# Latent attention: sine tables through DRAM in two transfers, its opening in one written order, four order lists as two blocks

## The chip, the cores and the metric

The kernel runs on one core of one Trainium2 chip. The metric is the device time of one execution in microseconds (us). The core has five engines that take their own instructions in order and wait for each other by semaphores: PE (TensorE, matmuls; its weight loads are listed as PEld), DVE (VectorE), ACT (ScalarE), POOL (GpSimd) and SP (SyncE, which only issues transfers). Transfers (DMAs) are issued here by SP and POOL and run on 16 DMA engines. Matmuls read SBUF and write PSUM, which has eight banks.

## What is computed

One layer of a streaming encoder. The part at hand is multi-head latent attention over 1024 prompt rows and 32 sample rows, 8 heads, cut from the reference:

```
q = (rms_norm(q_lat, g_q_lat) @ w_uq).reshape(B, T, H_A, NOPE + ROPE)      # 384 -> 8 x (64 + 32)
q_rope = apply_rope(q[..., NOPE:], cos[:, None, :], sin[:, None, :])
k_rope = apply_rope(k_r, cos, sin)
k_nope, v = c_kv @ w_uk, c_kv @ w_uv                                       # 256 -> 8 x 64 each
s = (einsum('bqhd,bshd->bhqs', q_nope, k_nope) + einsum('bqhr,bsr->bhqs', q_rope, k_rope)) * 96 ** -0.5
mask = (kpos[None, :] // 64) <= (qpos[:, None] // 64)
p = softmax(where(mask, s, -1e30)); o = einsum('bhqs,bshd->bqhd', p, v)
```

Stick-breaking attention, its projection `o_b @ w_proj_b`, the gates, the merge and a convolutional feed-forward follow or stand around it. Every product of float32 operands is made of three matmuls (`mm3`): each operand is split into a high half, written by ACT (`hi`, L68), and a low half, the rest, written by DVE (`lo`, L71), and high·high, low·high and high·low are added in PSUM.

## The kernel before

**Stages.** `run` calls the stages in turn: projections, stick-breaking attention (`stage_sb`), the latents (`stage_lat`, L1243), latent attention (`stage_mla`, L1378), merge, feed-forward. A planner orders each engine's instructions by data, free buffers and its own estimate of durations. Inside a `manual_schedule` region the engines named there keep the order in which the code issues; SP and POOL stay with the planner.

**Latents.** `lat_rstd` (L1201) works out 1/rms of the query latent, sends it to DRAM and back as nine columns (`cols`, five transfers on POOL, L1218 and L1220), by which the scores' exponentials are scaled. The key rope rows are rotated and spread over `KRp` in twelve pieces (L1355, POOL).

**Opening of `stage_mla`.** The scaled cosine and sine tables are loaded into `tc` and `KSm`, 128 partitions of four equal parts, by twelve SP transfers (L1385, L1387). For head pair 0, `expansion(p)` returns steps: `I`/`i` split the weights; `z` (nine steps) makes the rotary products of four heads, `B` (six) multiplies them by the tables (L1446) and sends them to DRAM (`rqc`, `rqs`, L1448), from where rows of each head come back (L1455) into its query tile; `x` (nine) makes the other query products and `X`/`K` copy them (L1465 on DVE, L1463 on ACT); `y` (four) makes the keys, `H`/`L` their high and low halves, alternating between the two heads; `J`/`j` are the query tile's high half QH and low half QL (L1469, L1473); `Z` copies the sample's columns. `values` makes the value tiles of four heads. `proj_b` is the other branch's projection, done meanwhile: `O` splits its input `ob`, `U` loads a weight, `W`/`w` split it, `f` is a fill of three matmuls, `G` stores a result. All this opening is outside a manual region: the planner orders it.

**The four blocks.** `mla_attend` (L898) plays one list of items per head pair in a manual region for PE, ACT and DVE: `ORDER_0`, `ORDER_A`, `ORDER_A`, `ORDER_L` for pairs 0 to 3. An item is a letter and a place: in `S2.1a`, 2 is the unit (0 to 3 are the blocks of 256 rows of the pair's first head, 4 to 7 those of the second in falling size), 1 its half of 128 rows, `a` a part of the keys. `S` scores (one of three PSUM banks), `M`, `m`, `n` the scaled maximum, `E` the exponential into a row tile (five buffers), `s`, `R`, `C` or `c` the normalisation, `T` the turn (transposes to one of two banks), `h`, `v` its halves, `V` weights by values (one bank), `o`, `p` the output. Letters alone are fills: those of `proj_b`, and those of the next pair's expansion, so that each list ends with its last keys and queries. Pair 3 has the sample's attention (`Y`) and the split of its output (`q`, `r`). Between pairs 1 and 2 the planner orders the sample's latents and the values of the second four heads.

Of the kernel before, what the change touches and what calls it, by code (L numbers as in the profile page):

```python
# [44 lines left out]
class K:  # L45
# [777 lines left out]
    def sb_weights(self, pieces, w):  # L823
# [26 lines left out]
    ORDER_0 = """  # L850
        S0.0 S0.1 S1.0 W f M0.0 n0.0 f M0.1 n0.1 M1.0 n1.0 f E0.0 f E0.1 w f E1.0 S1.1 G R0.0 R0.1 R1.0 c0.0
        S2.0a C0.1 c1.0 M1.1 n1.1 S2.0b M2.0a T0.0 E1.1 f M2.0b h0.0 f R1.1 m2.0 C1.1 E2.0a f v0.0 E2.0b S2.1a G
        s2.0 S2.1b R2.0 M2.1a c2.0 V0.0 M2.1b S3.0a o0 m2.1 E2.1a p0 T1.1 M3.0a E2.1b T1.0 f s2.1 R2.1 W S3.0b
        C2.1 h1.1 S3.1a w h1.0 v1.1 f2 v1.0 f M3.0b V1.1 G M3.1a V1.0 T2.2 m3.0 o1 T2.1 E3.0a p1 f h2.2 f h2.1
        v2.2 f E3.0b S3.1b v2.1 V2.2 s3.0 M3.1b T2.0 R3.0 V2.1 m3.1 c3.0 S4.0a h2.0 f M4.0a E3.1a f v2.0 f G f
        E3.1b S4.0b s3.1 R3.1 V2.0 C3.1 S4.1a o2 M4.0b f p2 T3.3 m4.0 M4.1a G T3.2 E4.0a f h3.3 f h3.2 v3.3 f
        E4.0b S4.1b v3.2 V3.3 s4.0 M4.1b T3.1 R4.0 V3.2 m4.1 c4.0 S5.0a h3.1 T3.0 M5.0a f E4.1a v3.1 f I f2 V3.1
        S5.0b G i h3.0 f2 E4.1b f G f v3.0 z z z B B z z z B B z z z B B x s4.1 S5.1a M5.0b R4.1 m5.0 V3.0 C4.1
        E5.0a x E5.0b M5.1a x o3 s5.0 p3 T4.3 R5.0 T4.2 X K c5.0 S5.1b h4.3 S6.0 h4.2 M5.1b x v4.3 x v4.2 T4.1
        m5.1 M6.0 n6.0 E5.1a V4.3 h4.1 V4.2 E5.1b x v4.1 E6.0 T4.0 s5.1 X K f R5.1 R6.0 W V4.1 C5.1 S6.1 G w  # L860
        h4.0 T5.2 c6.0 v4.0 S7.0 h5.2 x M6.1 n6.1 T5.1 v5.2 E6.1 V4.0 M7.0 n7.0 h5.1 x R6.1 C6.1 o4 T5.0 v5.1
        E7.0 x h5.0 p4 S7.1 R7.0 X K c7.0 y v5.0 J V5.2 M7.1 n7.1 V5.1 Z E7.1 j V5.0 T6.1 o5 T6.0 h6.1 R7.1 p5 y
        C7.1 h6.0 v6.1 v6.0 H H L V6.1 V6.0 L T7.0 o6 h7.0 p6 v7.0 y V7.0 y o7 p7 H H L L Z J j
    """.split()

    ORDER_A = """
        S0.0 S0.1 S1.0 W f M0.0 n0.0 f M0.1 n0.1 M1.0 n1.0 f E0.0 f E0.1 w f E1.0 S1.1 G R0.0 R0.1 R1.0 c0.0
        S2.0a C0.1 c1.0 M1.1 n1.1 S2.0b M2.0a T0.0 E1.1 f M2.0b h0.0 f R1.1 m2.0 C1.1 E2.0a f v0.0 E2.0b S2.1a G
        s2.0 S2.1b R2.0 M2.1a c2.0 V0.0 M2.1b S3.0a o0 m2.1 E2.1a p0 T1.1 M3.0a E2.1b T1.0 f s2.1 R2.1 W S3.0b
        C2.1 h1.1 S3.1a w h1.0 v1.1 f2 v1.0 f M3.0b V1.1 G M3.1a V1.0 T2.2 m3.0 o1 T2.1 E3.0a p1 f h2.2 f h2.1  # L870
        v2.2 f E3.0b S3.1b v2.1 V2.2 s3.0 M3.1b T2.0 R3.0 V2.1 m3.1 c3.0 S4.0a h2.0 f M4.0a E3.1a f v2.0 f G f
        E3.1b S4.0b s3.1 R3.1 V2.0 C3.1 S4.1a o2 M4.0b f p2 T3.3 m4.0 M4.1a G T3.2 E4.0a f h3.3 f h3.2 v3.3 f
        E4.0b S4.1b v3.2 V3.3 s4.0 M4.1b T3.1 R4.0 V3.2 m4.1 c4.0 S5.0a h3.1 T3.0 M5.0a f E4.1a v3.1 f I f2 V3.1
        S5.0b G i h3.0 f2 E4.1b f G f v3.0 x s4.1 S5.1a M5.0b R4.1 m5.0 V3.0 C4.1 E5.0a x E5.0b M5.1a x o3 s5.0
        p3 T4.3 R5.0 T4.2 X K c5.0 S5.1b h4.3 S6.0 h4.2 M5.1b x v4.3 x v4.2 T4.1 m5.1 M6.0 n6.0 E5.1a V4.3 h4.1
        V4.2 E5.1b x v4.1 E6.0 T4.0 s5.1 X K f R5.1 R6.0 W V4.1 C5.1 S6.1 G w h4.0 T5.2 c6.0 v4.0 S7.0 h5.2 x
        M6.1 n6.1 T5.1 v5.2 E6.1 V4.0 M7.0 n7.0 h5.1 x R6.1 C6.1 o4 T5.0 v5.1 E7.0 x h5.0 p4 S7.1 R7.0 X K c7.0
        y v5.0 J V5.2 M7.1 n7.1 V5.1 Z E7.1 j V5.0 T6.1 o5 T6.0 h6.1 R7.1 p5 y C7.1 h6.0 v6.1 v6.0 H H L V6.1
        V6.0 L T7.0 o6 h7.0 p6 v7.0 y V7.0 y o7 p7 H H L L Z J j
    """.split()  # L880

    ORDER_L = """
        S0.0 S0.1 S1.0 W f M0.0 n0.0 f M1.0 n1.0 f M0.1 n0.1 E0.0 f E1.0 w f E0.1 Y G S1.1 R0.0 R1.0 R0.1 Y C0.1
        S2.0a c0.0 c1.0 M1.1 n1.1 S2.0b M2.0a E1.1 Y M2.0b T0.0 Y R1.1 f m2.0 C1.1 S2.1a h0.0 E2.0a v0.0 f E2.0b
        Y M2.1a s2.0 R2.0 V0.0 c2.0 S2.1b Y T1.1 o0 M2.1b T1.0 h1.1 p0 S3.0a h1.0 m2.1 v1.1 f q v1.0 E2.1a f
        V1.1 r E2.1b M3.0a f G W Y s2.1 R2.1 C2.1 w V1.0 T2.2 o1 Y h2.2 p1 v2.2 q r T2.1 Y V2.2 h2.1 T2.0 v2.1 f
        Y f2 h2.0 Y V2.1 G S3.0b v2.0 S3.1a M3.0b Y m3.0 M3.1a E3.0a V2.0 E3.0b f2 o2 s3.0 S3.1b Y R3.0 p2 c3.0
        S4.0a M3.1b Y q f M4.0a Y f G r f m3.1 Y E3.1a E3.1b s3.1 R3.1 C3.1 S4.0b Y S4.1a M4.0b Y m4.0 M4.1a
        E4.0a T3.3 f Y E4.0b T3.2 h3.3 s4.0 S4.1b R4.0 h3.2 v3.3 c4.0 S5.0a v3.2 T3.1 M4.1b V3.3 h3.1 M5.0a V3.2
        m4.1 v3.1 f E4.1a T3.0 E4.1b f V3.1 h3.0 s4.1 R4.1 Y G C4.1 v3.0 T4.3 T4.2 h4.3 Y h4.2 v4.3 v4.2 V3.0 Y  # L890
        f o3 T4.1 p3 f Y f2 h4.1 V4.3 Y q V4.2 G v4.1 S5.0b Y r M5.0b T4.0 Y V4.1 m5.0 h4.0 S5.1a E5.0a v4.0 Y f
        E5.0b M5.1a f Y S5.1b s5.0 R5.0 c5.0 Y M5.1b m5.1 E5.1a E5.1b s5.1 V4.0 R5.1 Y C5.1 S6.0 o4 S6.1 p4 M6.0
        n6.0 q Y r E6.0 T5.2 M6.1 n6.1 S7.0 h5.2 Y f E6.1 R6.0 M7.0 n7.0 T5.1 v5.2 c6.0 f R6.1 C6.1 h5.1 T5.0
        V5.2 E7.0 v5.1 h5.0 S7.1 G R7.0 v5.0 T6.1 c7.0 f h6.1 M7.1 n7.1 V5.1 v6.1 E7.1 V5.0 R7.1 T6.0 C7.1 o5 f
        p5 h6.0 f q V6.1 v6.0 G T7.0 r V6.0 h7.0 o6 v7.0 p6 q V7.0 r o7 p7 q r
    """.split()

    def mla_attend(self, order, score, V, out, fill):  # L898
        nc, vec = self.nc, self.nc.vector
        tiles, banks, stats = {}, {}, {}  # L900
        common = self.sums(V, out, tiles)
        for x in order:
            k, x = x[0], x[1:]
            if k in "fGWwxyzXKBJjZHLIiYqr":
                for _ in range(int(x or 1)):
                    fill(k)
                continue
# [10 lines left out]
            if k == "S":  # L918
                if not j:
# [281 lines left out]
    def lat_rstd(self, ps, n, cols=None):  # L1201
# [14 lines left out]
        if cols is not None:  # L1216
            d = d.rearrange("q c -> (q c)")
            nc.gpsimd.dma_start(cols[:, :8], d[:TP].rearrange("(b p) -> p b", p=P))  # L1218
            for q in range(4):
                nc.gpsimd.dma_start(cols[32 * q : 32 * q + 32, 8:9], d[TP:].rearrange("(p b) -> p b", b=1))  # L1220
            return
# [21 lines left out]
    def stage_lat(self):  # L1243
# [13 lines left out]

        lp = self.tc.alloc_tile_pool(name="lt", bufs=2, reuse_waits="tile")
# [119 lines left out]
    def stage_mla(self):  # L1378
# [5 lines left out]
        for j in range(0, P, 32):  # L1384
            nc.sync.dma_start(tc_[j : j + 32], a["k_ropeq"][64:96])  # L1385
            for d in (0, 16):
                nc.sync.dma_start(ts_[j + d : j + d + 16], a["k_ropeq"][112 - d : 128 - d])  # L1387
# [7 lines left out]
        def expansion(p, banks="mm"):  # L1395
# [85 lines left out]
            def keys():  # L1481
                for c0 in (0, 512):
                    ps = self.bank(next(banks))
                    c = slice(c0, c0 + 512)
                    for e in range(2):
                        kb.append((ps[64 * e : 64 * e + 64], e, c))
# [4 lines left out]
            def k_high():  # L1491
                ps, e, c = kb[k_done[0]]
                k_done[0] += 1
                self.hi(KHs[e][0:64, c], ps)

            def k_low():
                ps, e, c = kb[k_done[1]]
                k_done[1] += 1
                self.lo(KLs[e][0:64, c], ps, KHs[e][0:64, c])

            k_done = [0, 0]
# [3 lines left out]
                        J=q_high, j=q_low, Z=q_sample, H=k_high, L=k_low), QH, QL  # L1505

        def values(hf, raw, gt):
# [3 lines left out]
            for t in range(0, 8, 2):  # L1511
                ps = self.bank(gt.split()[t // 2 % len(gt.split())])
                for j in range(2):
                    tk = slice((t + j) * P, (t + j + 1) * P)
                    for k in range(2):
                        self.mm3(ps[:, j * 256 : j * 256 + 256], self.CPh[k][:, tk], self.CPl[k][:, tk],
                                 h[:, k * 256 : k * 256 + 256], l[:, k * 256 : k * 256 + 256], k == 0, k == 1)
                pv = ps.rearrange("r (j q h d) -> r j q h d", j=2, q=2, h=2)
                for q in range(2):
# [32 lines left out]
        for k in "JjZ":  # L1552
            steps[k]()
# [1121 lines left out]
```

## Time and profile before

| | us |
|---|---|
| three runs: median (lowest, highest) | 1716.35 (1715.44, 1718.22) |
| the profiled execution | 1719.44 |
| its span, first to last instruction | 1717.7 |
| PE busy in the span | 1654.9 |
| first matmul of `stage_mla` | 571.87 after the span's start |
| first score of pair 0 | 600.66 |
| end of pair 3, as cut here | 861.20 |

Times in the profile count from the span's start. Ends of matmuls are modelled, so busy time of PE says little of its rate; the spacing of starts says more. A wait is put down to the instruction whose semaphore came last.

### The profile page before, as it was taken

To read this page: it belongs to the slowest core of one execution; us is meant where nothing else is said; L and a number is where in the kernel's file an instruction comes from. 1 tells how busy PE (TensorE), PEld (TensorE's weight loads), DVE (VectorE), ACT (ScalarE), POOL (GpSimd) and SP (SyncE) were. 2 spreads that over 40 slices of the span, in tenths; PEclk is the share of its full clock that TensorE was granted. 3 is DMA by queue.
4 is the path that set the end of the run, shared out by engine and by line. 5 is a ranking of instruction groups with operands and counts; after the bars stand their busy time and mean duration, and the time that the engine had idled before them with its cause. 6 is when DMAs were issued, how large, how long until landed. Compare 5 with 4: busy or idle time off the path is not lost. (4 is left out here: it accounts for less than half of the span.)

```text
span 1717.7 us, 30277 instructions
## 1 busy us (share of the span) xinstructions
PE 1654.9 (96%) x11592; PEld 1508.9 (88%) x11592; DVE 1273.6 (74%) x2140; ACT 1007.2 (59%) x1945; POOL 297.9 (17%) x578
## 2 busy tenths in 40 slices
PE   5999999999999798999999999999999999999997
PEld 3999999999998687897889789999999999977885
DVE  4865788988864568777776779887787787787455
ACT  4544687888865457777773476444444444544442
POOL 3113212121110411110100121211121111110013
PEclk8999999999999999999999999999999999999999
DMA  9345966576432623221274531423333333697643
GB/s 331 101 134 182 295 206 178 174 195 179 137 111 72 157 71 99 67 84 53 67 263 149 172 127 57 143 93 130 132 105 132 131 110 132 231 333 244 210 138 120
DMA packets 192849, 259.54 MB, mean 151 GB/s; under 512 B 22270, under 2 KB 131200, under 8 KB 192704
## 3 DMA queue, kind: packets, MB, share of 16 engines
q1 hardware_dynamic: 171888, 198.97, 37.3%
q0 software_dynamic: 20592, 58.55, 9.8%
q8 instruction: 91, 1.49, 0.4%
q14 instruction: 54, 0.44, 0.1%
q10 hardware_dynamic: 224, 0.09, 0.0%
HBM read 190.02 MB, written 66.74 MB: 149 GB/s over the span
## 5 line engine op out<-in xcount | busy, mean ns | idle before, releaser
L68 ACT ACTIVATE wh<-wr 128x1024 fp32r<-128x1024 f32 (+3 forms) x151 | 130.2, 864 | 229.6 <-PE s L2129 84.1
L71 DVE TENSOR_TENSOR wl<-wr,wh 128x1024 fp32r<-128x1024 f32 (+3 forms) x151 | 148.4, 986 | 83.4 <-ACT wh L68 80.8
L75 PE MATMUL mm<-hh,wh 128*128 128x352 f32 x456 | 152.6, 335 | 0.0
L76 PE MATMUL mm<-hl,wh 128*128 128x352 f32 x456 | 148.9, 327 | 0.4 <-DVE hl L333 0.4
L77 PE MATMUL mm<-hh,wl 128*128 128x352 f32 x456 | 148.4, 326 | 0.0
L2128 PE MATMUL mm<-T,wh 128*128 128x256 f32 (+1 forms) x376 | 108.1, 288 | 0.0
L2130 PE MATMUL mm<-T,wl 128*128 128x256 f32 (+1 forms) x376 | 107.1, 285 | 0.4 <-DVE wl L71 0.2
L2129 PE MATMUL mm<-T,wh 128*128 128x256 f32 (+1 forms) x376 | 106.6, 284 | 0.0
L2130 PE MATMUL s<-T,wl 128*128 128x256 f32 (+1 forms) x348 | 99.3, 285 | 0.0
L2128 PE MATMUL s<-T,wh 128*128 128x256 f32 (+1 forms) x348 | 99.2, 285 | 0.0
L2129 PE MATMUL s<-T,wh 128*128 128x256 f32 (+1 forms) x348 | 98.8, 284 | 0.0
L71 DVE TENSOR_TENSOR wl<-S,wh 128x1024 fp32r<-128x1024 f32 (+1 forms) x55 | 59.2, 1078 | 51.0 <-ACT wh L68 50.8
L76 PEld LDWEIGHTS mm<-hl,wh 128*128 128x128 f32 x456 | 86.6, 190 | 3.4 <-DVE hl L333 1.7
L2269 DVE SCALAR_TENSOR_TENSOR u<-u,c,u 128x1058 f32<-128x1058 f32 x68 | 87.0, 1317 | 3.4 <-ACT u L2266 2.1
L75 PEld LDWEIGHTS mm<-hh,wh 128*128 128x128 f32 x456 | 86.5, 190 | 3.3 <-issue 2.1
L806 PE MATMUL tr<-c,A 128*128 128x128 f32 x576 | 85.3, 273 | 2.1 <-DVE PTl L71 1.3
L77 PEld LDWEIGHTS mm<-hh,wl 128*128 128x128 f32 x456 | 86.4, 190 | 0.2
L68 ACT ACTIVATE wh<-S 128x1024 fp32r<-128x1024 f32 (+1 forms) x55 | 51.8, 943 | 48.7 <-PE s L2129 13.3
L934 ACT ACTIVATE A<-s,mx,lat 128x384 f32<-128x384 f32 (+5 forms) x96 | 64.1, 672 | 26.7 <-DVE mx L929 17.6
L2130 PE MATMUL tr<-T,wl 128*128 128x272 f32 (+1 forms) x272 | 77.7, 286 | 0.7 <-DVE wl L71 0.7
L2128 PE MATMUL tr<-T,wh 128*128 128x272 f32 (+1 forms) x272 | 77.8, 286 | 0.0
L2129 PE MATMUL tr<-T,wh 128*128 128x272 f32 (+1 forms) x272 | 77.3, 284 | 0.0
(768 smaller groups left out, 5805.5 us busy)
## 6 DMA issues: line engine op xcount, KB each, us to landing
wr<-in_w_up_dram SPq DMA_DIRECT2D x44, 512.0 KB, 4.1
dr<-in_w_down_dram SPq DMA_DIRECT2D x43, 512.0 KB, 5.2
wr<-in_w_in_dram SPq DMA_DIRECT2D x33, 512.0 KB, 6.7
A<-in_w_ada_dram SPq DMA_DIRECT2D x32, 512.0 KB, 6.1
wr<-gdn SPq DMA_DIRECT2D x30, 512.0 KB, 4.6
gdn<-u POOLq DMA_DIRECT2D x23, 512.0 KB, 5.2
gd<-nat POOLq DMA_DIRECT2D x48, 176.0 KB, 3.6
t<-gd SPq DMA_DIRECT2D x16, 528.0 KB, 6.3
```

What stands on the lines that cost most here:

```text
L68: self.nc.scalar.activation(out, in_, AF.Identity, scale=scale)
L71: return self.nc.vector.tensor_tensor(out, full, hi.bitcast(F32), ALU.subtract)
L75: m(ps, lh, rh, start=start, stop=False)
L76: m(ps, lh, rl, start=False, stop=False)
L77: self.pe = m(ps, ll, rh, start=False, stop=stop).ins
L806: self.nc.tensor.transpose(tr[:, (2 * s + q) * P : (2 * s + q + 1) * P], at[q][:, b * P : b * P + P], self.idt)
L934: self.exp = nc.scalar.activation(A[:, c0 : c0 + m], banks[x][:, :m], AF.Exp, bias=mx[:, 0:1], scale=self.qs[:, 2 * u + i : 2 * u + i + 1] ...
L2128: m(ps[:, :n], w[0][:, k], x[0][:, k, c], start=first and k == 0, stop=False, skip_group_check=True)
L2129: m(ps[:, :n], w[0][:, k], x[1][:, k, c], start=False, stop=False, skip_group_check=True)
L2130: i = m(ps[:, :n], w[1][:, k], x[0][:, k, c], start=False, stop=k == 3, skip_group_check=True)
L2269: nc.vector.scalar_tensor_tensor(y, u[:, w : w + YW], self.cvT[:, w, cc : cc + 1], y, ALU.mult, ALU.add)
```

## The change

1. *Tables.* In `stage_lat`, twelve POOL transfers write both tables from the constants to two DRAM tiles in the arrangement of `tc` and `KSm`; in `stage_mla` two SP transfers load them.
2. *Queues.* The five column transfers of `lat_rstd` and four of the twelve `KRp` pieces go from POOL to SP.
3. *Opening.* Its products stand in one manual region for PE, ACT and DVE: keys, rotary products, multiplications, queries, values alternating with the splits of `ob`, key rows, queries' halves. `values` and `O` return steps for that.
4. *Lists.* `ORDER_M` plays pairs 0 and 1, `ORDER_N` pairs 2 and 3; a digit ahead of an item names the pair. `mla_attend` keeps one set of tiles and banks for each pair. `D` begins the next expansion, `U`, `N`, `k` are loads that were tied to `w` and `i`. `H`/`L` serve the first head, `g`/`b` the second. The number of items of each kind is the same in both sets, apart from empty ones.

```diff
-    ORDER_0 = """
...
-        C7.1 h6.0 v6.1 v6.0 H H L V6.1 V6.0 L T7.0 o6 h7.0 p6 v7.0 y V7.0 y o7 p7 H H L L Z J j
...
+    ORDER_M = """
+        0S0.1 0M0.1 0n0.1 0S1.1 0E0.1 0S0.0 f4 W f 0M0.0 0n0.0 G 0M1.1 0n1.1 f2 w 0R0.1 0E1.1 f 0S1.0 0C0.1
...
+        0E3.1a 0T2.2 0h2.2 0S4.0a 0i G 0M4.0b 0z 0M4.0a 0o1 0z 0m4.0 0E3.1b 0s3.0 0E4.0a 0v2.2 0z 0z 0z 0R3.0
+        0s3.1 0T2.0 0h2.1 0B 0S4.1b 0h2.0 0B 0p1 0S4.1a 0V2.2 0E4.0b 0c3.0 0v2.1 0R3.1 W 0C3.1 0v2.0 0V2.1 0z
...
+        0R6.0 0H f 0E7.0 f 0T5.0 0p4 0C6.1 0c6.0 0L 0S7.1 0h5.0 0v5.1 0M7.1 0v5.0 0V5.2 0g 1S1.1 W 0T6.1 G 0n7.1
+        0V5.1 0h6.1 0R7.0 1M1.1 0b 1n1.1 0E7.1 0V5.0 0y 0o5 0T6.0 1E1.1 0c7.0 0v6.1 0h6.0 1S0.0 0p5 w 0y 1S1.0
+        1M0.0 f 0R7.1 0C7.1 0g 0V6.1 f 0H f 0T7.0 1S0.1 0v6.0 0V6.0 W 1n0.0 f 0b 1E0.0 1S2.0b 1M1.0 0L 1R0.0
+        1n1.0 f w 1M0.1 1n0.1 1c0.0 0h7.0 1M2.0b 1E1.0 0o6 f 0v7.0 0p6 1S2.0a 1E0.1 1M2.0a f 1R0.1 f 1R1.0 1m2.0
...
+    def mla_attend(self, order, lists):
         nc, vec = self.nc, self.nc.vector
-        tiles, banks, stats = {}, {}, {}
-        common = self.sums(V, out, tiles)
+        ctx = [None, None]
         for x in order:
+            p = 0
+            if x[0].isdigit():
+                p, x = int(x[0]), x[1:]
+            if ctx[p] is None:
+                score, V, out, fill = lists[p]()
+                tiles = {}
+                ctx[p] = score, fill, tiles, {}, {}, self.sums(V, out, tiles)
+            score, fill, tiles, banks, stats, common = ctx[p]
...
-            nc.gpsimd.dma_start(cols[:, :8], d[:TP].rearrange("(b p) -> p b", p=P))
+            nc.sync.dma_start(cols[:, :8], d[:TP].rearrange("(b p) -> p b", p=P))
             for q in range(4):
-                nc.gpsimd.dma_start(cols[32 * q : 32 * q + 32, 8:9], d[TP:].rearrange("(p b) -> p b", b=1))
+                nc.sync.dma_start(cols[32 * q : 32 * q + 32, 8:9], d[TP:].rearrange("(p b) -> p b", b=1))
...
+        self.rtd = [self.dr.tile([P, T], F32, name=n) for n in ("rtc", "rts")]
+        for j in range(0, P, 32):
+            for x, r, c, n in ((0, 0, 64, 32), (1, 0, 112, 16), (1, 16, 96, 16)):
+                with self.tc.issue_after(self.sum_ins):
+                    nc.gpsimd.dma_start(self.rtd[x][j + r : j + r + n], a["k_ropeq"][c : c + n])
...
-                nc.gpsimd.dma_start(KRp[r : r + n, TQ * q : TQ * q + w], kr[32 * q + d : 32 * q + d + n, :w])
+                (nc.sync if r == 96 else nc.gpsimd).dma_start(KRp[r : r + n, TQ * q : TQ * q + w], kr[32 * q + d : 32 * q + d + n, :w])
...
-        for j in range(0, P, 32):
-            nc.sync.dma_start(tc_[j : j + 32], a["k_ropeq"][64:96])
-            for d in (0, 16):
-                nc.sync.dma_start(ts_[j + d : j + d + 16], a["k_ropeq"][112 - d : 128 - d])
+        for x, d in zip((tc_, ts_), self.rtd):
+            nc.sync.dma_start(x, d)
...
-        for _ in range(3):
-            for k in "zzzBB":
+        Vs, vstep = values(0, raw, "mm s s")
+        for _ in "UU":
+            proj["U"]()
+        E = mybir.EngineType
+        with self.tc.manual_schedule(engines={E.PE, E.Activation, E.DVE}):
+            for k in "yyHgLbyyHgLbzzzzzzzzzBBBBBBxxxXKxxxXKxxxXK":
                 steps[k]()
-        for _ in range(2):
-            for k in "yyHHLL":
+            ob = proj["O"]()
+            for _ in vstep:
+                next(ob)
+            self.krope_out()
+            proj["W"]()
+            proj["w"]()
+            self.hi(KHs[0][64:128], self.KRp[64:128])
+            self.lo(KLs[0][64:128], self.KRp[64:128], KHs[0][64:128])
+            for x in (KHs, KLs):
+                nc.gpsimd.dma_start(x[1][64:128], x[0][64:128])
+            for k in "JjJjZZ":
                 steps[k]()
-        Vs = values(0, raw, "mm s s")
-        proj["O"]()
...
-        for k in "UUWwU":
-            proj[k]()
+        proj["U"]()
...
+        for b, order in enumerate((self.ORDER_M, self.ORDER_N)):
+            if b:
+                self.mla_sample_latents()
+                Vs, vstep = values(1, raws[1], "mm tr")
+                list(vstep)
+                proj["U"]()
+                list(proj["O"]())
+                for k in "UWwU":
+                    proj[k]()
             with self.tc.manual_schedule(engines={E.PE, E.Activation, E.DVE}):
-                self.mla_attend((self.ORDER_0, self.ORDER_A, self.ORDER_A, self.ORDER_L)[p], score, lambda b, h: Vs[p % 2][:, b, h], out, fill)
+                self.mla_attend(order, [lambda p=p, v=Vs: one(p, v) for p in (2 * b, 2 * b + 1)])
```

More of the change, by code (lines that the diff above doesn't have):

```diff
@@ L864 @@
-    """.split()
[L866 to L879, printed above, removed]
@@ L918, in mla_attend @@
             if k == "S":
-                if not j:
+                if t not in tiles:
                     tiles[t] = self.tl(self.At, [P, TP], F32, "A")
@@ L1484, in keys @@
                     c = slice(c0, c0 + 512)
-                    for e in range(2):
-                        kb.append((ps[64 * e : 64 * e + 64], e, c))
+                    kb.append((ps, c))
                     for k in range(2):
@@ L1549, in stage_mla @@
-        for x in (KHs, KLs):
-            nc.gpsimd.dma_start(x[1][64:128], x[0][64:128])
-        self.krope_out()
-        for k in "JjZ":
-            steps[k]()
-        for k in "UUWwU":
-            proj[k]()
-        for p in range(4):
-            if p == 2:
-                self.mla_sample_latents()
-                Vs = values(1, raw, "mm tr")
-                proj["U"]()
-                proj["O"]()
-            if p in (1, 2):
-                for k in "UWwU":
-                    proj[k]()
-            def score(e, ps, i, c0, n, last, QH=QH, QL=QL):
+        Vs, vstep = values(0, raw, "mm s s")
@@ new lines, in stage_mla, with expand, weights, cached @@
+        proj["U"]()
+        raws, nexts = {}, {}
+        def expand(p):
+            nexts[p], QHs[p + 1], QLs[p + 1] = expansion(p + 1)
+        def weights():
+            raws[1] = load_values(1)
+        def cached():
+            self.KSm, self.VSm = self.tl(M, [P, 2, KS], F32, "KSm"), self.tl(M, [P, 5, 256], F32, "VSm")
+            nc.sync.dma_start(self.VSm[:, :4], a["cache_mla_ckv"][0, 0].rearrange("(t p) c -> p t c", p=P))
+        o3, sample = [], []
+        def split(o, r, c):
+            self.hi(o3[0][r, c], o[r])
+            yield
+            self.lo(o3[1][r, c], o[r], o3[0][r, c])
@@ L1567, in score, with one @@
+        def one(p, Vs):
+            def score(e, ps, i, c0, n, last):
                 q, c = slice(i * P, (i + 1) * P), slice(c0, c0 + n)
                 m = nc.tensor.matmul
-                m(ps[:, :n], QH[e][:, q], KHs[e][:, c], start=True, stop=False)
-                m(ps[:, :n], QH[e][:, q], KLs[e][:, c], start=False, stop=False)
+                m(ps[:, :n], QHs[p][e][:, q], KHs[e][:, c], start=True, stop=False)
+                m(ps[:, :n], QHs[p][e][:, q], KLs[e][:, c], start=False, stop=False)
@@ L1573, in score @@
                     m(ps[:, d : d + 64], self.idb, self.mk64, start=False, stop=False)
-                m(ps[:, :n], QL[e][:, q], KHs[e][:, c], start=False, stop=True)
-            out = self.store(self.oad[p])
+                m(ps[:, :n], QLs[p][e][:, q], KHs[e][:, c], start=False, stop=True)
+            parts = []
+            out = self.store(self.oad[p]) if p < 3 else lambda *x: parts.append(split(*x))
             if p == 3:
                 v = self.tl(O, [P, 2 * T], F32R, "V")
-                o3 = v[:, :T], v[:, T:]
-                def split(o, r, c):
-                    self.hi(o3[0][r, c], o[r])
-                    yield
-                    self.lo(o3[1][r, c], o[r], o3[0][r, c])
-                def out(*x):
-                    parts.append(split(*x))
-                parts, sample = [], self.mla_sample(QZ, QR)
@@ L1621, in fill @@
                 elif k == "Y":
-                    next(sample)
+                    if not sample:
+                        sample.append(self.mla_sample(QZ, QR))
+                    next(sample[0])
                 elif k in "qr":
                     next(parts[0] if k == "q" else parts.pop(0), None)
-            E = mybir.EngineType
+                else:
+                    nexts[p][k]()
+            return score, lambda b, h: Vs[p % 2][:, b, h], out, fill
+        for b, order in enumerate((self.ORDER_M, self.ORDER_N)):
[7 more added lines that the diff above has]
+                    proj[k]()
@@ L1804, in operands, with steps @@
                 fetch()
-            for k in range(4):
-                f = fs.pop(0)
-                self.hi(ob[0][:, k], f)
-                self.lo(ob[1][:, k], f, ob[0][:, k])
+            def steps():
+                for k in range(4):
+                    f = fs.pop(0)
+                    self.hi(ob[0][:, k], f)
+                    self.lo(ob[1][:, k], f, ob[0][:, k])
+                    yield
+            return steps()
         def load():
```

172 lines of the change are left out of this document (92 added, 80 removed).

## The prediction

> **What bounds the kernel now.** I read the page first, then the busy time of each engine by stretches of the latent attention, then the list of what TensorE (PE) waited for there, and last the instructions in order of time around the longest wait.
>
> ```profile
> PE 1654.9 (96%) x11592; PEld 1508.9 (88%) x11592; DVE 1273.6 (74%) x2140; ACT 1007.2 (59%) x1945; POOL 297.9 (17%) x578
> ```
>
> PE is the bound over the whole, so the change can gain only where PE stands or runs slowly. Next, the stretches; the columns are the stretch, its length, busy time of each engine with its instructions, granted clock, DMA share and GB/s.
>
> ```profile
> 571.90:600.66 28.76, 18.99 (x122) 16.95 (x118) 16.41 (x36) 13.13 (x25) 15.99 (x31) 0.93 0.69 168
> 600.66:606.80 6.14, 5.75 (x24) 5.12 (x24) 4.60 (x10) 2.37 (x6) 0.00 (x0) 0.50 0.04 5
> 606.80:661.90 55.10, 51.12 (x352) 45.10 (x352) 38.96 (x102) 36.30 (x87) 7.17 (x13) 1.00 0.35 99
> 661.90:680.00 18.10, 14.60 (x94) 11.82 (x91) 15.81 (x40) 13.94 (x33) 2.51 (x5) 1.00 0.27 68
> 680.00:721.00 41.00, 40.06 (x283) 35.58 (x283) 31.48 (x78) 31.99 (x76) 6.21 (x12) 1.00 0.21 64
> 721.00:728.00 7.00, 5.60 (x35) 4.23 (x34) 6.74 (x15) 6.25 (x14) 1.05 (x2) 1.00 0.30 87
> 728.00:785.00 57.00, 56.22 (x405) 50.56 (x405) 45.84 (x119) 44.13 (x106) 7.67 (x14) 1.00 0.26 76
> 785.00:801.40 16.40, 12.70 (x74) 10.39 (x73) 13.65 (x31) 11.86 (x27) 2.14 (x4) 0.90 0.24 69
> 801.40:861.20 59.80, 59.16 (x412) 51.11 (x410) 41.85 (x111) 44.55 (x108) 5.46 (x11) 1.00 0.22 75
> sum 289.30, PE 264.20 PEld 230.86 DVE 215.33 ACT 204.51 POOL 48.20; mean PE 29.36 PEld 25.65 DVE 23.93 ACT 22.72 POOL 5.36
> ```
>
> In order: the opening, the first scores at half clock, head pair 0 (with the rotary products), the seam of pairs 0 and 1, pair 1, the seam in the middle (the second half's values), pair 2, the seam of pairs 2 and 3, pair 3. PE idles 289.30 − 264.20 = 25.1 us: 9.8 in the opening, 4.0 in pair 0, 3.5 and 3.7 at the two seams that the change dissolves, 1.4 at the one it keeps, 2.7 in all the rest. Inside the pairs little is left: 0.9 of 41.0 us, 0.8 of 57.0. Half clock costs half of 5.75, 2.9 us, in the second row, and 0.10 × 16.4, 1.6 us, in the eighth.
>
> ```profile
> PE s L1569 <- ACT QH L68: 6.3, 1, 6.3
> PE mm L75 <- DVE KL L71: 5.5, 3, 2.5
> PE mm L75 <- DVE big L1446: 3.1, 3, 1.1
> PE pv L820 <- DVE o L794: 2.1, 3, 0.9
> ```
>
> These are PE's waits (total, times, longest). The first is the opening's, of the second one (next keys' low halves) 4.4 us fall on the seams, the third is the rotary products of pair 0, the fourth again the seams. The work that the change rearranges is thus what PE waits for.
>
> **The opening, as it is.** Its instructions in order of time (start, length, engine and line, tiles, count, idle before and who ended it):
>
> ```profile
> 571.87 0.43 PE L75 MATMUL mm<-lat,wh 128*128 128x352 f32 x1
> 579.13 0.49 PE L1361 MATMUL tr<-c,big 128*128 128x128 f32 x3
> 580.70 0.36 PE L75 MATMUL mm<-wh,lat 128*128 128x256 f32 x1 [1.09 <-DVE KL L71]
> 583.50 0.28 PE L77 MATMUL s<-wh,lat 128*128 128x256 f32 x1
> 587.82 0.40 PE L75 MATMUL mm<-lat,wh 128*128 128x352 f32 x1 [0.48 <-DVE V L71]
> 589.18 0.32 PE L77 MATMUL mm<-lat,wl 128*128 128x352 f32 x1
> 590.33 0.52 DVE L1446 TENSOR_TENSOR VSm<-mm,tc 128x352 f32<-128x352 f32 x1
> 593.03 0.32 SPq L1448 DMA_DIRECT2D rqs<-big  x1
> 596.96 0.32 SPq L1455 DMA_DIRECT2D big<-rqs  x1
> 599.55 1.06 ACT L68 ACTIVATE QH<-big 128x1024 fp32r<-128x1024 f32 x1 [2.29 <-DMA big<-rqs]
> 600.64 1.23 DVE L71 TENSOR_TENSOR QL<-big,QH 128x1024 fp32r<-128x1024 f32 x1 [0.90 <-ACT QH L68]
> 601.92 0.58 PE L1574 MATMUL s<-KH,QL 128*128 128x256 f32 x1 [0.39 <-DVE QL L71]
> ```
>
> Rotary and key products leave PE between 571.87 and 579.13 (39 matmuls, 7.26 us), yet their first multiplication by the tables runs at 590.33: DVE had the keys' and values' low halves ahead of it. Not the tables are late: the twelve pieces went out until 576.5 and took 4.5 us.
>
> ```profile
> L1387 SPq DMA_DIRECT2D KSm<-in_k_ropeq_dram x8: 311/418/428, 572.0 to 576.5; - x8
> DMA to landing us min/median/max: 3.1/4.5/4.9
> 577.05 2.83 SPq L1799 DMA_DIRECT2D A<-ob  x4
> t<-gd SPq DMA_DIRECT2D x16, 528.0 KB, 6.3
> ```
>
> So two transfers in place of twelve free the sync queue (SP) for the `ob` fetch about 4 us earlier, but do not by themselves advance the multiplications; the new order does.
>
> **The change, step by step.** (1) *The opening.* PE: keys and rotary 7.26, then the queries, 27 by 0.17 (nine start within 589.18 − 587.82 and one spacing), the values, 48 by 0.12 (24 within 583.50 − 580.70 and one), and the three transposes 0.5: 571.9 + 18.1 = 590.0. Query rows: the last rotary product ends at 579.1, its two multiplications (0.52 each) at 580.2; out and back as now, 596.96 − 593.03 = 3.9 and 599.55 − 596.96 = 2.6, then QH 1.06: 587.8. DVE does, from the first key halves to the end of QL, what one stretch counts:
>
> ```profile
> 573.60:601.90 28.30, 18.16 (x111) 15.89 (x110) 16.07 (x31) 13.13 (x25) 14.96 (x29) 0.91 0.70 168
> ```
>
> It can begin when six key matmuls (of 0.23) and a high half (0.6) are done, 574.0, and with its 16.1 us ends at 590.1 without a pause; I allow 1.3 of pauses, since ACT's high half stands ahead of each low one: 591.4. DVE is last; PE's 590.0 covers the rest, and what is late next is the low half QL. It now ends at 600.64 + 1.23 = 601.9: 10.5 us less at best. Table rows weigh against that: the second table waits for its bytes until 572.0 (the first start of its row) and needs, at 528 KB, up to 6.3 us: 578.3, just in time. But five column loads and four key pieces now go through SP too, and if the planner keeps them ahead, 9 × 0.42 (the median of that row) = 3.8 us later: 582.1, multiplications until 585, QL by 595. I take −9 (between −6 and −10). Off POOL's queue go the same nine, which helps the key rows and ends nothing on PE's path.
>
> (2) *Half clock at the first scores*, −2.9 if the new wait (590.0 to 591.4, 1.4 us) keeps the clock, 0 if not; at the seam of pairs 2 and 3, −1.6 or 0. I take −3.5 for both.
>
> ```profile
> 796.87 0.36 PE L75 MATMUL mm<-ObH,wh 128*128 128x264 f32 x1 [2.46 <-DVE KL L71]
> ```
>
> A stop of 2.46 us was enough there for the lower clock of the eighth stretch. [...]
>
> (3) *Rotary products of pair 1*, in pair 0: three `z` and two `B` alternate with nothing between, and the groups wait about 1.05 each (3.1, three times, above). In the new list scores, turns and exponentials stand between them. −2.8 of 3.1; 0 at worst.
>
> (4) *Two seams dissolved.* Head 0's next keys (`H`, `L`) now come as soon as head 0's scores are done, and pair 1's first scores stand among pair 0's last turns and values. Idle 3.5 and 3.7; I take −2.7 each, and −1 each as the poor end. The seam in the middle stays, 1.4.
>
> (5) *New waits.* The same matmuls, halves and copies remain (I counted both sets of lists: 96 scores, 80 turns, 80 value groups, 128 fills, 32 sample steps in each set). Between the last score of a pair of rows and its turn the old list has at least 4.2 us of PE work, the new 5.0 in the first block; between a turn and its values 0.7 and 1.4. Only the first turn of the second block has less, 2.9. The scarce things are one bank for values and five row tiles; in the new lists a score sometimes stands ahead of the turn that frees the fifth. Fewest waits 0, most: the rate of the worst present stretch outside seams, 4.0 of 55.1, over 260 us, 19. I take +3, near pairs 1 and 2, whose lists are of this kind.
>
> (6) *Twelve table writes* from DRAM to DRAM on POOL. They are to be issued behind a DVE instruction, which orders nothing on POOL, and they wait for no data; a load without a wait goes early in this program:
>
> ```profile
> 491.11 0.54 SPq L1329 DMA_DIRECT2D wk<-in_w_in_dram  x1
> 564.16 0.16 PEld L1343 LDWEIGHTS mm<-hh,wk 128*32 128x32 f32 x8 [0.21 <-issue]
> 10.00:20.00 10.00, 7.34 (x56) 2.79 (x56) 3.01 (x4) 1.15 (x2) 3.37 (x6) 1.00 1.05 377
> 573.82 2.02 POOL L1220 DMA_DIRECT2D lat<-lr  x4
> ```
>
> `wk` goes 73 us before its use. Placed in the kernel's first 40 us, where the DMA engines are full, 1.08 MB take 2.9 us at the row's 377 GB/s; anywhere else the 12 × 0.5 us lie in POOL's idle time and cost 0. I take +1.
>
> Sum: −9.0 − 3.5 − 2.8 − 5.4 + 3 + 1 = −16.7. The profiled execution took 1719.44 us (span 1717.7 and 1.7 around it), 0.18% above the median of the three runs, 1716.35; taken from that median, the forecast is 1699.6.
>
> **Rivals.** *Only the opening pays* (1704.5): terms 1 and 2's first part, −11.9, while the lists give back what the seams gain. For it: inside the pairs PE is busy 97.7% to 98.9% already, and a list in one order can move a wait rather than end it. Against: the seams' 7.2 us come from dependences that the split of `H`/`L` by head removes. *Only the lists pay* (about 1708): SP holds the tables behind the nine moved loads, and the first score comes no more than 2 us earlier, with half clock; −2 − 2.8 − 5.4 − 1.6 + 3 + 1 = −7.8, rounded. Against: its rows allow 582.1 at worst. *The blocks lose DVE's order* (1725, slower): DVE has 198.9 us of work in the 260.5 after 600.66, 76%, and takes it strictly in order. If in the mixed lists an item whose input is late stands ahead of the low half of a turn, PE's values wait; 80 turns by 0.25 us is 20, so −11.9 + 20 + 1 = +9. It decides once the blocks take over 273 us, DVE's share below 73%. For it: pair 1's seam has DVE at 15.81 of 18.10 already. Against: more PE work lies between turn and values. *The change doesn't do what it says* (1716): tables early, multiplications still late, lists even.
>
> **How the numbers follow.** Forecast (−12 to −25) 0.58; only the opening 0.17; only the lists 0.07; no effect 0.05; slower 0.13. A measurement here can tell about 0.2%, 3.4 us. Faster 0.82, same 0.05, slower 0.13. Best of all terms is idle 25.1 and clock 4.5: 1686.8, so the range begins at 1687; it ends at 1716, which leaves out the slower case and little else. The forecast's own range is 1691 to 1705.
>
> **What would show it.** First score near 591 rather than 600.66, with the clock at 1.00 to the end of the stage; multiplications at L1446 in one run of six before 585; no wait of PE for `KL` over 1 us beyond the opening; PE's idle time in the stage near 10 us; POOL's twelve writes and their place. Wrong: a first score after 597, half clock in the blocks, PE's waits for the turns' low halves above 6 us in sum, or DVE below 73% in the blocks.

## The result and the profile after

The changed kernel takes 1706.57 us (median of 4, 1706.11 to 1707.33) beside 1717.01 for the kernel before on the same chip: ratio 0.994, 95% interval 0.9923 to 0.9957. A repeat (e12 below) gave 0.9922 (0.9901 to 0.9943). So it is faster, by 10.4 us where 16.7 were forecast. The profiled execution took 1706.11 (span 1704.3, 13.4 less than before).

The page's line of busy times, and PE's longest waits between 560 and 860 us (total, times, longest):

```profile
PE 1648.0 (97%) x11592; PEld 1512.1 (89%) x11592; DVE 1268.7 (74%) x2140; ACT 1008.8 (59%) x1945; POOL 303.9 (18%) x581
...
PE s L1612 <- ACT QH L68: 8.2, 1, 8.2
PE mm L75 <- ACT KH L68: 4.6, 1, 4.6
PE s L1612 <- ACT A L961: 3.6, 2, 2.0
PE s L75 <- DVE big L1476: 1.4, 1, 1.4
PE s L75 <- ACT big L1493: 1.4, 1, 1.4
...
```

The seams' waits (4.4 of the 5.5 for `KL`, 2.1 for `o`) and those of pair 1's rotary products (3.1) are gone. The opening's wait for `QH` is longer, 8.2 instead of 6.3, and a new one of 4.6 stands for `KH`, which is not the keys' tile any more here but the operand of the merge's projection that takes its place. The stretches (length; PE, PEld, DVE, ACT, POOL; clock, DMA share, GB/s) show where they lie:

```profile
571.98:601.70 29.72, 18.66 (x125) 17.03 (x118) 16.11 (x32) 11.51 (x25) 8.32 (x18) 0.94 0.40 123
601.70:608.60 6.90, 6.34 (x25) 5.40 (x26) 6.10 (x15) 2.50 (x4) 2.82 (x6) 0.50 0.53 118
608.60:722.00 113.40, 113.26 (x829) 104.95 (x829) 96.68 (x245) 95.19 (x220) 17.52 (x32) 1.00 0.33 96
722.00:728.10 6.10, 4.07 (x20) 3.63 (x19) 4.46 (x16) 4.19 (x11) 0.00 (x0) 0.72 0.22 86
728.10:776.30 48.20, 48.00 (x350) 44.20 (x350) 38.33 (x98) 39.64 (x91) 7.11 (x14) 1.00 0.24 70
776.30:782.70 6.40, 4.79 (x26) 4.50 (x26) 4.68 (x11) 4.66 (x12) 1.64 (x3) 0.73 0.13 41
782.70:844.80 62.10, 61.92 (x435) 54.16 (x435) 46.43 (x126) 49.44 (x121) 6.07 (x12) 1.00 0.14 46
844.80:854.40 9.60, 4.97 (x19) 4.48 (x17) 3.65 (x3) 4.09 (x4) 0.34 (x7) 0.64 0.96 364
```

Inside the blocks PE idles 0.14 of 113.40, 0.20 of 48.20, 0.18 of 62.10 us: almost nothing, apart from two stops (fourth and sixth row). The opening is no shorter than before: 29.4 us from its first product (572.30) to the first score, where it was 28.8. At the merge's start, the last row, PE idles 4.6 us and then runs slowly, with the granted clock at 0.50 until 854.

The opening in order of time, from four engines:

```profile
572.30 0.50 PE L75 MATMUL mm<-lat,wh 128*128 128x512 f32 x1
575.61 2.47 SPq L1387 DMA_DIRECT2D A<-big  x4
578.18 0.52 SPq L1417 DMA_DIRECT2D KSm<-rts  x1
583.51 0.52 DVE L1476 TENSOR_TENSOR big<-s,KSm 128x352 f32<-128x352 f32 x1 [4.93 <-DMA KSm<-rts]
589.50 0.46 ACT L1493 ACTIVATE big<-s 64x352 f32<-64x352 f32 x1 [12.90 <-DMA rqs<-big]
593.59 0.38 ACT L1552 ACTIVATE V<-s 128x256 fp32r<-128x256 f32 x1 [0.83 <-DVE V L71]
600.59 2.00 ACT L68 ACTIVATE QH<-big 128x1024 fp32r<-128x1024 f32 x2
```

The moved loads stand ahead of the second table on SP, so it leaves at 578.18 and VectorE (DVE) stands still for 4.93 us. ScalarE (ACT) stands still for 12.90 before its first query copy, for a buffer of the tag `big` (there are three of them): `krope_out`'s transposes now come after the values and hold one. Behind that copy stand, in ACT's order, all value groups and the high halves of the queries.

And the merge's start, in the changed kernel and in the one before (last copy of the sample's rows, last loads of the attention's rows, first operand's high half):

```profile
841.92 0.46 DVE L1792 COPY os<-tr 64x64 f32<-64x64 f32 x2
844.65 0.84 SPq L1666 DMA_DIRECT2D big<-oa  x2
848.63 1.08 ACT L68 ACTIVATE KH<-big 128x1056 fp32r<-128x1056 f32 x1 [4.55 <-DMA big<-oa]
```

```profile
851.80 0.45 DVE L1765 COPY os<-tr 64x64 f32<-64x64 f32 x2
854.34 0.81 SPq L1639 DMA_DIRECT2D big<-oa  x2
```

The loads need what the sample's last step stores. Before, that step came three microseconds ahead of the last score's record (854.80); now it stands at the very end of the second block, eight behind it (833.90).

### The profile page after: what moved, and what is told of

It is laid out like the page before. It is cut to its first block, busy times and chain, and to the rows that moved or that the text cites. A ratio compares the mean times of both kernels' runs of the same rounds, so it can differ in the third digit from the quotient of the medians.

```text
span 1704.3 us, 30277 instructions
## 1 busy us (share of the span) xinstructions
PE 1648.0 (97%) x11592; PEld 1512.1 (89%) x11592; DVE 1268.7 (74%) x2140; ACT 1008.8 (59%) x1945; POOL 303.9 (18%) x581
## 5 line engine op out<-in xcount | busy, mean ns | idle before, releaser
L806 PEld LDWEIGHTS tr<-c,A 128*128 128x128 f32 x576 | 69.3, 140 | 3.9 <-PE tr L806 0.4
```

Source lines behind the costliest of these rows:

```text
L806: self.nc.tensor.transpose(tr[:, (2 * s + q) * P : (2 * s + q + 1) * P], at[q][:, b * P : b * P + P], self.idt)
```

## The experiments

Each was timed beside the kernel before. "Score" is the time from the first matmul of `stage_mla` to the first score, in the profiled execution.

| run | us | ratio (95%) | score |
|---|---|---|---|
| before | 1717.01 | | 28.8 |
| changed | 1706.57 | 0.994 (0.9923 to 0.9957) | 29.4 |
| e1 transposes early | 1702.56 | 0.9912 (0.9898 to 0.9926) | 25.3 |
| e2 nine loads on POOL | 1702.27 | 0.9913 (0.9897 to 0.9928) | 24.7 |
| e3 both | 1703.66 | 0.9923 (0.991 to 0.9936) | 27.5 |
| e4 lists alone | 1702.48 | 0.991 (0.9891 to 0.993) | 28.1 |
| e5 table writes late | 1704.52 | 0.9924 (0.9908 to 0.9939) | 28.6 |
| e6 e1, values skewed | 1697.22 | 0.9883 (0.9867 to 0.99) | 22.4 |
| e7 sample early | 1702.11 | 0.9906 (0.9889 to 0.9924) | 28.7 |
| e8 opening rearranged | 1699.78 | 0.99 (0.9883 to 0.9917) | 25.0 |
| e9 e5 + e6 + e7 | 1692.39 | 0.9855 (0.9842 to 0.9869) | 22.6 |
| e10 e9, tables first | 1691.15 | 0.9847 (0.9834 to 0.9861) | 21.3 |
| e11 opening alone | 1719.79 | 1.0015 (1.0002 to 1.0027) | 28.9 |
| e12 changed, again | 1704.78 | 0.9922 (0.9901 to 0.9943) | 29.2 |

### Which part gained: e4, e11, e12

e4 has the new lists, with opening, tables and queues as before. e11 has the old lists, with everything else as changed.

> The changed kernel with its opening and its tables as before: twelve table pieces straight to SBUF, the nine loads on POOL, keys, values and queries of the opening in the planner's order. Only the two blocks of lists are new. Theory (the lists alone made the gain, the opening and the tables cost something): first score near 600.7, last score 22 us earlier than before, 8 to 9 of it given back at the merge: 1702 to 1705.5. Rival (the opening did pay, hidden in the scores after it): the gain from first to last score shrinks by 5 us or more, 1709 or more.

> The kernel before with the change's tables, its moved loads and its opening order, but the four old lists. Theory (the opening as written saves nothing: its first score comes 0.8 us later after the last matmul of the rotated keys than before, and the table writes delay the start by 2 to 3 us): 1717.5 to 1721. Rival (the opening pays on its own and only the new lists hide it): 1714 or less.

> The changed kernel itself, run again beside e11. Theory: its ratio to the kernel before stays at 0.994, 1705 to 1708.5, so that e4 (lists alone, 0.991) is the faster of the two and the opening and the tables cost 3 to 5 us of it. Rival (the difference to e4 was the scatter of the runs): 0.9915 or less, 1703 or less.

The lists alone give 0.991, the rest alone 1.0015, with an interval that lies just above 1: the opening with its tables loses 2.3 us by the medians, and at least does not gain. The product of the two, 0.9925, agrees with e12's 0.9922. e12 itself fell between its theory (0.994) and its rival (0.9915 or less), so that e4 is faster than the changed kernel by more than scatter is not shown: their intervals overlap.

### What holds the opening: e1, e2, e3

e1 moves one call ahead; e2 puts the columns (the first line of them is shown) and the four key pieces back on POOL:

```diff
+            self.krope_out()
+            for k in "BBBBBBxxxXKxxxXKxxxXK":
...
-            self.krope_out()
...
-            nc.sync.dma_start(cols[:, :8], d[:TP].rearrange("(b p) -> p b", p=P))
+            nc.gpsimd.dma_start(cols[:, :8], d[:TP].rearrange("(b p) -> p b", p=P))
```

> The changed kernel, with the three transposes that read the rotated keys issued right after the rotary products instead of after the values; nothing else moves. Theory (the third big buffer): the transposes hold that buffer until 592.97, so the query copies on ScalarE find no buffer and wait 12.90 us (576.60 to 589.50). With the buffer free early this wait falls to the table chain alone (multiplications until 585.8): query copies near 585, first score 594 to 596 instead of 601.70, time 6 to 9 us less, 1698 to 1701. Rival (the late second table sets the first score, the buffer is only the next in line): first score after 599.5, time at most 2 us less, 1704.5 or more.

> The changed kernel, with the five column loads and four key pieces back on the POOL queue. Theory (both waits in a chain): the second table's load starts at about 572 instead of 578.18, VectorE's wait of 4.93 us goes, the products of the tables leave 4 to 5 us earlier, and as ScalarE's wait ends with their store, so does it: first score about 597, time 3 to 5 us less, 1701.5 to 1703.5. Rival (the buffer alone sets it): VectorE's wait goes, but ScalarE waits until about 589 as before and the first score stays within 1 us of 601.70, time within 1.5 us of 1706.6.

> Both edits: the transposes early and the nine loads back on POOL. Theory: neither wait is left, first score 590 to 593 as the opening's term forecast, no half clock at the first scores if PE's stop there stays under 2.4 us; 10 to 14 us less than the changed kernel, 1692.5 to 1697. Rival (the merge takes back what comes early, as it took 8.5 us of the lists' gain): the first score comes 10 us earlier, but the end only 3 to 6, 1700.5 to 1703.5.

In e1, the last reads of the rotated keys, DVE's first copy of the queries, ACT's first, and the high halves; in e2, the first product with the second table and ACT's first copy; in e3, the reads and the copy that waits for them:

```profile
578.72 1.46 POOL L1389 DMA_DIRECT2D lat<-big  x3
585.69 0.51 DVE L1495 TENSOR_SCALAR big<-s 64x352 f32<-64x352 f32 x1
586.23 0.46 ACT L1493 ACTIVATE big<-s 64x352 f32<-64x352 f32 x1 [5.09 <-DMA out_dram<-nat]
597.05 2.00 ACT L68 ACTIVATE QH<-big 128x1024 fp32r<-128x1024 f32 x2
```

```profile
579.05 0.51 DVE L1476 TENSOR_TENSOR big<-s,KSm 128x352 f32<-128x352 f32 x1
585.40 0.46 ACT L1493 ACTIVATE big<-s 64x352 f32<-64x352 f32 x1 [8.24 <-DMA rqs<-big]
```

```profile
584.20 1.46 POOL L1389 DMA_DIRECT2D lat<-big  x3 [0.69 <-DMA A<-big]
586.96 0.46 ACT L1493 ACTIVATE big<-s 64x352 f32<-64x352 f32 x1 [7.50 <-DMA lat<-big]
```

e1 and e2 each shorten the opening by four to five microseconds. They are two ways into one wait: e1 frees the third buffer, e2 sends out earlier the store (`rqs`) that frees another. Both rivals fall. e1's first score, 598.2, is later than its theory had it (594 to 596): its query copy now follows DVE's copy from the same bank (585.69), which stands right behind the late multiplications, so the table is what is left of the wait. e3 does not add the two, and its theory fell: with twelve key pieces and five columns on POOL, the last three reads of the rotated keys go out at 584.20 instead of 578.72, the same buffer is held by them, and ACT waits 7.50. Its 2.4 us for the clock was the author's estimate from the stop of 2.46 in the prediction; PE's stop ahead of e3's first score was 8.2, and in the changed kernel half clock came behind two shorter than 2.4 (last section). Its rival was wrong too, since the loss is in the opening (27.5 us to the first score, where e1 and e2 have 25) and not at the merge.

In e1, e2 and e3 alike 10.7 to 11.1 us pass from the first query copy to the first high half, whatever came before: a second cause, which the next runs take up.

### The values' turns: e6, e8

e6 is e1 with the halves of `ob` between the two halves of each value group; e8 puts them ahead of the queries, with the key rows ahead of the values, and halves the values in pairs over two banks; it also has the transposes early, the tables ahead of the moved loads, the columns back on POOL and eight key pieces on SP. From the edit of e6:

```diff
-                    yield
+                        yield
...
-            for _ in vstep:
-                next(ob)
...
+            for i, _ in enumerate(vstep):
+                if i % 2 == 0:
+                    next(ob)
```

> The kernel of e1, with the four high and low halves of ob put between the two halves of each value group, so that ScalarE has other work while VectorE reads the group's bank. Theory (from the query copies on, ScalarE's own queue sets the first score: 586.2 to 597.0 in e1, 2.02 us for each of four value groups because the two engines take turns on one bank): a group takes about 1.55 us, the first score comes 1.5 to 2 us earlier than in e1 (597.2 to 597.8 by the fourth matmul's record, e1 had 599.59), time 1700 to 1701.5. Rival (the query rows from DRAM set it): the first score does not move by more than 0.5 us, time as e1's 1702.6.

> The changed kernel with all that the opening was found to wait for set right together: tables ahead of the moved loads (columns on POOL, eight key pieces on SP behind the tables), the transposes early, the halves of ob and of the key rows ahead of the values in ScalarE's and VectorE's order, values halved in pairs over two banks. Theory (term 1's size was right and its cover was missing): PE runs from the rotary products to the end of the values with little wait, first score 591 to 594 (the fourth matmul's record; the changed kernel had 603.13), 8 to 11 us less, 1695 to 1698.5. Rival (what comes early is given back in the first rows of the list, where the loads and copies then come late): first score near 593, but the time no better than e1's and e2's 1702.4.

ACT in e6 (first query copy, first value half, a half of `ob`, the queries' high halves), then in e8:

```profile
584.01 0.46 ACT L1493 ACTIVATE big<-s 64x352 f32<-64x352 f32 x1 [4.70 <-DVE big L1495]
585.36 0.39 ACT L1552 ACTIVATE V<-mm 128x256 fp32r<-128x256 f32 x1
585.64 0.64 ACT L68 ACTIVATE ObH<-A 128x528 fp32r<-128x528 f32 x1
592.35 2.00 ACT L68 ACTIVATE QH<-big 128x1024 fp32r<-128x1024 f32 x2
```

```profile
583.26 1.32 ACT L68 ACTIVATE ObH<-A 128x528 fp32r<-128x528 f32 x2 [2.47 <-DMA A<-ob]
589.39 0.46 ACT L1498 ACTIVATE big<-s 64x352 f32<-64x352 f32 x1 [1.20 <-DMA out_dram<-nat]
```

In the changed kernel the second half of a group waits 0.83 for DVE's low half of the first (0.49 in the first group): both read one bank, and in the rows they take turns there, DVE's low half from 593.14 to 593.56 and ACT's second half from 593.59. With other work in that gap the stretch from query copy to high half falls from 10.82 (e1) to 8.34, and the kernel gains 5.3 us on e1, more than the 1 to 2.6 expected; 3.0 of it show in the opening, 1.7 ahead of it, where executions of one code differ by as much (L241, which no edit has touched, begins at 221.6 in e1 and at 219.8 in e6). e8 fell short, and neither its theory nor its rival gives the reason: `ob` comes late, and ACT, in its strict order, waits 2.47 for its first two pieces and 2.26 for the other two ahead of the query copy, which begins at 589.39.

### The merge: e7

Three of the sample's 32 steps (`Y`) move up, the last one from the end of `ORDER_N` to just before `1T5.0 1S7.0` (pieces of the lines):

```diff
- ... 1V7.0 f 1o7 1Y f 1p7 G 1r 1q 1r
+ ... 1V7.0 f 1o7 f 1p7 G 1r 1q 1r
- ... 1v5.1 1T5.0 1S7.0 ...
+ ... 1v5.1 1Y 1T5.0 1S7.0 ...
```

> The changed kernel, with only the last three steps of the sample rows in the second block moved ahead: the last one from the end of the list to just before the last pair of scores. Theory (the merge waits for these: the last two loads of the attention's rows go out at 844.65, 2.7 us after the last step at 841.92, and PE then waits 4.79 us and runs 6.8 us at half clock): loads out before 835, the wait for KH under 1 us, the merge's first matmul of the sample rows near 860 instead of 867.0; time 6 to 8.5 us less, 1698 to 1700.5. Rival (the merge is held by something else, such as the KH buffer that is free only after the last score, or the copies before it): the loads go out earlier but the wait shrinks by less than half, time 1704 or more.

```profile
835.42 0.45 DVE L1790 COPY os<-tr 64x64 f32<-64x64 f32 x2
838.05 0.81 SPq L1664 DMA_DIRECT2D big<-oa  x2
...
L1917 PE MATMUL pv<-dh,gs x16: 379/391/404, 863.4 to 867.2; 128*32 128x256 f32 x16
```

The loads go out 6.6 us earlier though the block began 0.3 later, the wait for `KH` is gone from PE's list, and the merge's first sample product comes at 863.4 instead of 867.0. From the first score it is 261.4 us instead of 265.3, 3.9 less. The time is 4.5 us less than the changed kernel's, or 2.7 by its repeat e12, less than was expected; the last step still came after 835, but that this is the reason is not shown.

### The table writes: e5

```diff
-                    out(res[n], r, slice(u * 256, u * 256 + 256))
+                    self.stored = out(res[n], r, slice(u * 256, u * 256 + 256))
...
-                with self.tc.issue_after(self.sum_ins):
+                with self.tc.issue_after(self.stored.ins):
```

> The changed kernel, with the twelve table writes on POOL held behind the last store of the earlier attention stage (an instruction of POOL's own queue), so that they can't run in the first 40 us. Theory (the writes take DMA time from the loads that the start waits for): the L241 matmuls begin 2 to 3 us earlier (220.47 in the changed kernel; 219.5 to 221.6 in the three runs with early writes, 216.0 and 218.0 in the two without), time 1.5 to 3 us less, 1703.5 to 1705. Rival (absorbed before the latent attention, where the changed kernel was only 0.42 us behind): time within 1 us of 1706.6.

The first write and the group of matmuls after the kernel's start, in the changed kernel, then in e5:

```profile
12.56 0.55 POOL L1289 DMA_DIRECT2D rtc<-in_k_ropeq_dram  x1
...
L241 PE MATMUL mm<-A,cT x32: 379/379/403, 220.5 to 222.0; 128*32 128x256 f32 x32
```

```profile
498.95 0.52 POOL L1289 DMA_DIRECT2D rtc<-in_k_ropeq_dram  x1
...
L241 PE MATMUL mm<-A,cT x32: 379/379/403, 215.8 to 217.3; 128*32 128x256 f32 x32
```

The five profiled executions without early writes (before, e4, e5, e9, e10) begin L241 at 215.6 to 218.0, mean 216.2; the nine with them at 219.3 to 221.6, mean 220.3. The traces thus put the cost at 4 us. The medians do not resolve it: e5 is 2 us below the changed kernel and level with e12.

### Together: e9, e10

e10 adds to e9 that the nine loads follow the tables on SP, and that the first head's query halves stand ahead of the projection's weights.

```diff
-            nc.sync.dma_start(x, d)
+            table = nc.sync.dma_start(x, d).ins
+        with self.tc.issue_after(table):
+            self.krope_rows()
+            self.columns()
...
```

> The edits of e5 (table writes late), e6 (transposes early, value halves skewed) and e7 (last sample steps early) in one kernel. Theory (three separate places: start, opening, merge): their gains over the changed kernel add, about 2, 9 and 5 us; time 1689 to 1693. Rival (what comes early in one place waits in the next): no better than e6 alone by more than 2 us, 1695 or more.

> The kernel of e9, with the nine moved loads still on SP but behind the two table loads, and the halves for the projection's first weights behind the first head's query halves. Theory (with the buffer free and the values skewed, the table is the next late thing: e6's query copies began at 584.01, PE having waited 0.39 us for the multiplications): the second table goes out at about 572 to 573 instead of 578, the multiplications end by 582, query copies begin near 582.8 and the first score comes 1.5 to 2.5 us earlier than in e9, time 1687 to 1691.5. Rival (the key rows, now later, or the reads of the rotated keys take its place): first score within 0.7 us of e9's, time within 1 us of it.

```profile
569.52 0.34 SPq L1421 DMA_DIRECT2D KSm<-rts  x1
577.31 0.52 DVE L1483 TENSOR_TENSOR big<-s,KSm 128x352 f32<-128x352 f32 x1
579.61 0.46 ACT L1500 ACTIVATE big<-s 64x352 f32<-64x352 f32 x1 [2.01 <-DMA A<-big]
590.67 0.39 PE L1624 MATMUL s<-KH,QH 128*128 128x256 f32 x1 [3.57 <-ACT QH L68]
```

The gains of the three places add in e9, within scatter: 14.2 us less than the changed kernel, where e5, e6 and e7 alone sum to 15.9. In e10 the second table leaves before the keys' halves are done, the last multiplication begins at 577.31, and the opening is 21.3 us, 1.3 less than e9's and a little short of what was expected. The time is 1.2 less, within scatter, so this last step is shown by the trace alone. Either is faster than both kernels: e10 takes 1691.15 us beside 1717.53, and the list as changed stands in it unaltered but for three steps.

## Why the prediction was right, and where not

The sign and the range held, and so did the gain of the lists; the opening, forecast as the largest term, paid nothing. What came about is nearest to the rival that was given 0.07, "only the lists pay", at 1708. That the total still fell into the range (1687 to 1716) is in part luck: the range was wide, and the blocks gained more than forecast where the opening gained nothing. The forecast's own range, 1691 to 1705, was missed by 1.6 us; the repeat, at 1704.78, lies just inside. Two of the four signs that the prediction gave for being wrong appeared: a first score after 597 (601.70), and half clock in the blocks (0.72 and 0.73).

1. *The opening* (−9): +0.6 by the profile, and e11's loss. The step that failed is "DVE is last": 16.1 us of its work from 574.0 with 1.3 of pauses. DVE had pauses of 4.93 and 4.07, and at the first score PE waited 8.2 us for ACT, then only 0.6 for DVE. Three things were missing. SP did hold the second table behind the moved loads; the prediction saw this possibility, at 582.1 (it was 583.5), but ended `QL` at 595 by it. The third `big` buffer was not counted, though moving the transposes behind the values was plain in the change. And the copies, value halves and query halves were summed as if ACT and DVE ran side by side, where they take turns on a bank (the waits of 0.83 at e6). That most of the size was possible e10 shows: 21.3 us to the first score, 7.5 less than before, where the forecast had 9.
2. *Half clock* (−3.5): the second of its two parts came, the first did not; the row of the first scores still has 0.50, behind a stop of 8.2. That a stop of 1.4 us there would keep the clock was the author's estimate, and no run shows it: the shortest ahead of the first scores was 3.1, in e8. In the changed kernel's opening two stops of 1.45 and 1.37 left the clock at 1.00 (583 to 593 us). Three rows with 0.72, 0.73 and 0.64 came in addition, so the term came out as a loss.
3. *Rotary products* (−2.8): right; no wait for them stands inside the blocks.
4. *Seams* (−5.4): right in kind; both waits went entirely.
5. *New waits* (+3): right in size, 3.6, but in two stops for a row's exponentials (L961), at the kept middle seam and 54 us after it, not as small pieces. What was under-sized is the other side: the old small waits for `PTl`, `PTh` and `KH` were left standing in the sum, and the blocks ended them too. From the first score to the merge's first sample product the kernel takes 265.3 us (867.0 − 601.7) instead of 278.7 (879.4 − 600.7): −13.4, where terms 2 to 5 make −8.7. The stretch before, then changed:

```profile
600.66:879.40 278.74, 262.47 (x1768) 230.25 (x1768) 214.03 (x521) 202.49 (x465) 32.66 (x67) 0.98 0.27 84
601.70:867.00 265.30, 255.96 (x1768) 233.73 (x1768) 209.25 (x525) 205.08 (x466) 35.50 (x73) 0.96 0.30 91
```

For the same 1768 matmuls PE idles 9.3 us instead of 16.3, and is busy 6.5 less although the granted clock is lower. The prediction priced idle time and clock alone. As the ends of matmuls are modelled, a part of each stop can count as busy, and there are fewer stops now; that this makes the 6.5 is not shown. And 3.9 more were lost at the merge, by e7. That place was not in the prediction at all: the sample's 32 steps were counted, and where the last one stands was not asked.

6. *Table writes* (+1): they were hoisted as foreseen; their price was beyond the upper bound of 2.9 by the traces. That bound priced bytes on the DMA engines; POOL's own queue was forgotten, where twelve issues of half a microsecond stand between its small operations:

```profile
10.00:20.00 10.00, 6.54 (x46) 2.18 (x46) 3.01 (x4) 1.15 (x2) 7.68 (x15) 1.00 1.05 379
```

POOL is busy 7.68 of these 10 us, before 3.37. Which of the two, bytes or queue, makes the 4 us was not separated. The traces hint at both: the first L296 product, ahead of which PE waits 1.61 for a load (before, 0.75), begins at 24.98 instead of 22.82, and PE's wait for `hh` (L329) ends at 40.71 instead of 36.03, 4.7 later, while POOL sends three of the writes between its small operations.

The rival of the lost order on DVE did not occur: DVE is busy 96.68 of 113.40 us in the first block, 85%, and in both blocks PE waits 0.2 us for it.

## What to carry to other kernels

When a stretch is written in one order for several engines, list for each engine what must be free before its first instruction, buffers too: one late buffer at the head of a strict queue delays all behind it (here ACT's copies, values and halves, by a wait of 12.90 us), and moving a reader back is moving a release back. After a list is rewritten, look for the step whose result is loaded again by the next stage, and put it where the load is hidden. Two fixes for one wait need not add (27.5 us to the first score in e3, 25.3 and 24.7 in e1 and e2): ask first what a third user of the same buffer does.

## What the runs showed of the hardware

A stop of PE well below the one of 2.46 us in the prediction was followed by half clock, and another of the same length was not. In the changed kernel the two waits for L961 (3.6 in all: 2.03, which ended at 724.42, and 1.61, which ended at 778.28) are each followed by slow rows, 0.72 and 0.73 above; in steps of 1 us the granted clock was 0.50 from 725 to 728 and from 780 to 782. In e6 they are of about the same length, and in the row after the shorter one, 1.61, which ended at 770.23, the clock stays:

```profile
PE s L1615 <- ACT A L961: 3.5, 2, 1.9
...
772.00:776.00 4.00, 4.00 (x31) 3.53 (x31) 3.97 (x11) 3.32 (x10) 1.09 (x2) 1.00 0.30 89
```

In the kernel before, a stop of 1.93 us, which ended at 673.41, was followed by 1.00 as well (670 to 680 us). What decides it, these runs do not show.
